# Sums of squares over the partitions on 32-column tiles and in two steps, and six token sums issued ahead of the first projection

## The chip, the cores and the metric

The kernel runs on one core of a Trainium2 chip. The metric is the device time of one execution in microseconds. In the profile PE is TensorE's matmuls, PEld its weight loads, DVE is VectorE, ACT ScalarE, POOL GpSimd and SP the engine that issues most transfers. All engines run their own queue in order and wait for each other through semaphores.

## The reference, cut to what matters

Two blocks work on 512 tokens of width 1024. The first ends in a mixture of experts whose result is added to the residual h, and then in a norm over each token; the second begins with another norm, scaled and shifted by a vector that depends on a conditioning input, and a projection. At the seam:

```python
    h = h + hier_moe(n2, ...)              # last expert unit adds its part to h
    x = rms_norm(h, final_gain)            # first block's result
    # second block, layer 0
    h2 = rms_norm_2(x, norm_g, 1e-6) * (1.0 + scale) + shift
    b_gate, c_gate, xin, z = split(h2 @ conv_w_in, 4)
```

Both norms need, for every token, a sum of squares over the 1024 features. The kernel forms the second block's input by features (features on the partitions, tokens along the free axis), so that sum runs over the 128 partitions and over eight tiles (k = 0 to 7) of 128 features each.

## The kernel before, in words

The experts are worked off in 14 units. `unit(p)` gathers tokens, runs gate, up and down matmuls, and leaves a result `O` as a high and a low part (`OT[p]`). `spread(p, t, a)` brings it back to tokens: two matmuls of 512 columns into a PSUM bank for token tile t (of 4) and half a (of 2) of the width. `add_o(a)(t, ps)`, line 692, adds that bank to `h` on DVE. For most units `combine` does all eight.

The last unit is treated otherwise. `entering`, called as its tail, does not wait for `h`: for each k a bank `HB[k]` holds the turned `h` (`so_far`, line 1276) and gets the unit's part by two more matmuls. ACT squares it with a gain into `WQ` (wq, line 1300), DVE scales it into `HS` (hs, line 1301). Behind every fourth k `first_high` has ACT cast the next projection's weights to their high part (hi, line 1321). HS and WQ are two tiles of four k each.

Then, in the body, the sum of squares over partitions: for each k and each token tile one matmul with a 128 x 128 block of WQ as the weights and a single column of ones moving, 32 in all, into four columns of one bank `pc`. DVE adds a small constant (ss, line 1429), POOL raises to the power -0.5 (line 1430), PE turns the result across the partitions (line 1433). `first_low` has DVE make the low part of the first weights (lo, line 1325).

The loop over k then multiplies hs by that factor (hs, line 1438), has ACT shift it and round it to a high part (ah, line 1439), has DVE make the low part (al, line 1440), and issues twelve matmuls: two weight tiles g, two halves m, and for each the three products high x high, high x low, low x high. In the trace they read ah,hi then al,hi then ah,lo. The four banks `ps01` collect over all k. At k = 4 and k = 6 `emit_split(2)` casts the weights of the next two jobs in two pieces each (hi on ACT line 127, lo on DVE line 128).

The order of the work is the order of the code: every engine's queue is filled as the lines are reached. `residual` is a task of small steps that `drive` runs between later matmuls; before the change it issues all eight `spread` and `add_o` of the last unit, squares h for the first block's norm and scales it. The POOL queue also issues the loads of w_mod (wm, line 367).

Of the kernel before, what the change touches and what calls it, by code (L numbers as in the profile page):

```python
# [11 lines left out]
F32 = mybir.dt.float32  # L12
# [3 lines left out]
AF = mybir.ActivationFunctionType  # L16
OP = mybir.AluOpType
# [4 lines left out]
KT = D // 128  # L22
NT = S // 128
# [7 lines left out]
NU = len(SIZES)  # L31
# [21 lines left out]
def kernel(  # L53
# [9 lines left out]
    V, A, P, T = nc.vector, nc.scalar, nc.gpsimd, nc.tensor  # L63
# [48 lines left out]
    def emit_split(cuts=1):  # L112

        j = at["split"]
        while at["load"] <= j:
            emit_load()
        _, shape, cut = specs[j]
        at["split"] = j + 1
        if cut:
            raw = loaded.pop(j)  # L120
            hi = W(shape, F32R, name="hi")
            lo = W(shape, F32R, name="lo")
            parts[j] = (hi, lo)
            n = shape[1] // cuts
            for a in range(cuts):
                r = slice(a * n, (a + 1) * n)
                A.activation(hi[:, r], raw[:, r], AF.Copy)  # L127
                V.tensor_tensor(lo[:, r], raw[:, r], hi[:, r].bitcast(F32), op=OP.subtract)  # L128
                if a == cuts - 1:
                    free(raw)  # L130
                yield
# [43 lines left out]
    h = cp.tile([128, NT, D], F32, name="h")  # L175
# [20 lines left out]
    ones = cp.tile([128, NE], F32, name="ones")  # L196
# [212 lines left out]
    def load_row(src):  # L409
        t = W([128, 2, D], name="row")  # L410
        nc.scalar.dma_start(t[:, 0, :], src.to_broadcast([128, D]))
        return t
# [277 lines left out]
    def add_o(c):  # L690
        def add(t, ps):
            V.tensor_tensor(h[:, t, c * 512:(c + 1) * 512], h[:, t, c * 512:(c + 1) * 512], ps, op=OP.add)  # L692
        return add
# [423 lines left out]
    def spread(p, t, a):  # L1117
        pb = bank()
        for n in range(2):
            mm(pb, OHT[p][:, t * 128:(t + 1) * 128], OT[p][n][:, a * 512:(a + 1) * 512], n == 0, n == 1)  # L1120
        return pb
# [157 lines left out]
    def entry_gains():  # L1279

        g = cols[:, FG:FG + 8]
        V.tensor_tensor(ent[:, 0, :], g, mods[0][1], op=OP.mult)
        V.tensor_tensor(ent[:, 1, :], g, g, op=OP.mult)
        V.tensor_scalar(ent[:, 1, :], ent[:, 1, :], EPS, 1.0 / D, op0=OP.add, op1=OP.mult)
        V.memset(ent[:, 2, :], 0.5)
        P.tensor_tensor(ent[:, 1, :], ent[:, 1, :], ent[:, 2, :], op=OP.pow)  # L1286

    def entering(p, half):

        if half == 0:  # L1290
            HS.extend(W([128, 4, 512], name="hs") for _ in range(2))
            WQ.extend(W([128, 4, 512], name="wq") for _ in range(2))
            return
        O = OT[p][2]
        for k in range(KT):
            if k not in HB:
                so_far((k,))
            for n in range(2):
                mm(HB[k], O[:, n, k * 128:(k + 1) * 128], OHT[p], False, n == 1)
            A.activation(WQ[k // 4][:, k % 4, :], HB[k], AF.Square, scale=ent[:, 1, k:k + 1])  # L1300
            V.tensor_scalar(HS[k // 4][:, k % 4, :], HB.pop(k), ent[:, 0, k:k + 1], None, op0=OP.mult)
            if k % 4 == 3:
                first_high(k // 4)

    def turned(t, x_t, r, shift, order=False):

# [7 lines left out]
    def first_high(n):  # L1314

        j = j_c[0][n]
        while at["load"] <= j:
            emit_load()
        raw, hi, lo = loaded.pop(j), W(specs[j][1], F32R, name="hi"), W(specs[j][1], F32R, name="lo")
        firsts.append((hi, lo, raw))  # L1320
        A.activation(hi, raw, AF.Copy)

    def first_low(n, r):
        hi, lo, raw = firsts[n]
        V.tensor_tensor(lo[:, r], raw[:, r], hi[:, r].bitcast(F32), op=OP.subtract)  # L1325
        if r.stop == KT:
            free(raw)
# [94 lines left out]
            free(hi, lo)  # L1422


    pc = bank()
    for k in range(KT):
        for t in range(NT):
            mm(pc[:, t:t + 1], WQ[k // 4][:, k % 4, t * 128:(t + 1) * 128], ones[:, 0:1], k + t == 0, k + t == KT + NT - 2)
    V.tensor_scalar(ss0[:, 0, 0:NT], pc[:, 0:NT], EPS * EPS, None, op0=OP.add)
    P.tensor_tensor(ss0[:, 0, 0:NT], ss0[:, 0, 0:NT], mhalf[:, :NT], op=OP.pow)  # L1430
    pr = bank()
    for t in range(NT):
        T.transpose(pr[:, t * 128:(t + 1) * 128], bc(ss0[:, 0, t:t + 1], [128, 128]), ident)
    first_low(0, slice(0, 4))
    for k in range(KT):
        x_, sh = HS[k // 4][:, k % 4, :], mods[0][0][:, k:k + 1]
        hi, lo = hT[k]
        V.tensor_tensor(x_, x_, pr, op=OP.mult)  # L1438
        A.activation(hi, x_, AF.Identity, bias=sh)  # L1439
        V.scalar_tensor_tensor(lo, x_, sh, hi.bitcast(F32), op0=OP.add, op1=OP.subtract)  # L1440
        if k in (0, 2, 4):
            first_low(*((1, slice(0, 4)), (0, slice(4, 8)), (1, slice(4, 8)))[k // 2])
        for g in range(2):
            for m in range(2):
                if k == 0:
                    ps01[g, m] = bank()
                c = slice(m * 128, (m + 1) * 128)
                w = firsts[g]
                for n, (l, r) in enumerate(passes([(w[0][:, k, c], w[1][:, k, c], hi, lo)])):
                    mm(ps01[g, m], l, r, k + n == 0, k == KT - 1 and n == 2)  # L1450
        if k in (4, 6):
            for _ in emit_split(2):
                pass
    for g in range(2):
        for m in range(2):
            ev01[g](m, ps01[g, m])
        free(*firsts[g][:2])
    free(*HS, *WQ)

    def residual():  # L1460

        p = NU - 1
        fg = load_row(final_gain[None, :])
        for t in range(NT):
            for a in range(2):
                add_o(a)(t, spread(p, t, a))
            square(h[:, t, :], ss0[:, 1, t:t + 1], D ** -0.5)
            yield
        free(OT.pop(p)[2])
        s, r = ss0[:, 1, 0:NT], ss0[:, 2, 0:NT]  # L1470
        P.tensor_scalar(s, s, EPS, None, op0=OP.add)
        P.tensor_tensor(r, s, mhalf[:, :NT], op=OP.pow)
        for t in range(NT):
            for a in range(2):
                yield
                c = slice(a * 512, (a + 1) * 512)
                V.scalar_tensor_tensor(h[:, t, c], h[:, t, c], r[:, t:t + 1], fg[:, 0, c], op0=OP.mult, op1=OP.mult)
        free(fg)
# [377 lines left out]
```

## Time and profile before

| what | value |
|---|---|
| median of 3 runs | 1481.9 us (1480.66 to 1482.22) |
| profiled execution, its own time | 1482.14 us |
| its span, first to last instruction | 1480.5 us |
| mean granted clock of TensorE | 0.978 |
| PE, PEld busy | 95%, 68% of the span |
| DVE, ACT, POOL busy | 51%, 31%, 11% |

The time is 1.64 us longer than the span; an edit inside leaves that part alone. A share is a mean over stages with different limits, so the table says only that PE is hardly ever without work. What a change is worth at one place is read from the rows of that place: what starts when, and what released it. The clock is given as a share of 2.4 GHz and has two levels, 1.00 and 0.50.

### The profile page before, as it was taken

The numbers are of one execution on the slowest core, as the hardware profiler recorded it, in microseconds if no ns is written. First come the engines' busy times: TensorE is split into PE (matmuls) and PEld (weight loads), VectorE is DVE, ScalarE is ACT, GpSimd is POOL, SyncE is SP. The second block draws the span as 40 slices with busy tenths as digits, with TensorE's granted clock in tenths as the row PEclk, the third lists the DMA queues.
The fourth block names the chain that finished last, engine by engine and source line by source line (L and its number), as shares of the span: only waits on it lengthen the run. The fifth ranks groups of instructions, "written<-read, shape, count | busy, mean of one in ns | idle before, by whom it ended". The sixth has DMA issues, their size and how long they took to land.

```text
span 1480.5 us, 19691 instructions
## 1 busy us (share of the span) xinstructions
PE 1408.9 (95%) x7919; PEld 1012.6 (68%) x7919; DVE 758.9 (51%) x1276; ACT 463.5 (31%) x656; POOL 160.5 (11%) x179
## 2 busy tenths in 40 slices
PE   6997999898999889998989999999999999999998
PEld 5876788452544234452568888888888888888876
DVE  5787746743352323242358666664444444444535
ACT  4434314220111011110233212324453453453442
POOL 1035303100000000000010000013102102112101
PEclk9999999999999899999979999999999999999999
DMA  8532563799999999999935653143123122113011
GB/s 300 192 142 87 175 256 131 318 360 420 419 420 419 419 416 420 408 418 419 359 113 175 204 170 128 57 143 105 39 61 110 54 85 90 58 58 114 30 43 58
DMA packets 102567, 310.66 MB, mean 210 GB/s; under 512 B 5128, under 2 KB 59044, under 8 KB 77892
## 3 DMA queue, kind: packets, MB, share of 16 engines
q1 hardware_dynamic: 94612, 281.36, 49.9%
q0 software_dynamic: 6704, 25.34, 4.8%
q10 hardware_dynamic: 1152, 2.62, 0.5%
q8 instruction: 64, 1.05, 0.3%
q14 instruction: 35, 0.29, 0.1%
HBM read 307.20 MB, written 2.10 MB: 209 GB/s over the span
## 4 chain that ended last, share of the span: by engine, by line
PE 54%; issue 3%; DMA 2%; DVE 2%; ACT 1%; POOL 0%; POOLq 0%; SPq 0%; DVEq 0%
PE ps L90 53%; DMA ld<-in_w_down_dram 1%; DMA ld<-in_w_up_dram 1%; PE ps L1685 1%; DVE lo L128 1%; ACT ah L1439 0%; DVE hs L1438 0%; ACT hi L127 0%; DVE lo L1325 0%; PE ps L247 0%; DVE al L1440 0%; PE ps L406 0%; PE ps L1088 0%; POOL ss L1430 0%; POOL ent L1286 0%
## 5 line engine op out<-in xcount | busy, mean ns | idle before, releaser
L90 PE MATMUL ps<-ah,hi 128*128 128x512 f32 (+1 forms) x800 | 311.7, 390 | 2.1 <-ACT ah L1439 2.1
L90 PE MATMUL ps<-al,hi 128*128 128x512 f32 (+1 forms) x800 | 306.4, 383 | 0.3 <-DVE al L1440 0.3
L90 PE MATMUL ps<-ah,lo 128*128 128x512 f32 (+1 forms) x800 | 306.2, 383 | 0.0
L90 PE MATMUL ps<-ld,XT 128*64 128x512 f32 (+1 forms) x1088 | 210.3, 614 | 14.9 <-DMA ld<-in_w_up_dram 7.8
L128 DVE TENSOR_TENSOR lo<-ld,hi 128x2048 fp32r<-128x2048 f32 (+1 forms) x73 | 161.0, 2214 | 47.7 <-ACT hi L127 47.7
L90 PEld LDWEIGHTS ps<-ah,hi 128*128 128x128 f32 x800 | 151.2, 189 | 33.5 <-issue 3.2
L90 PEld LDWEIGHTS ps<-ah,lo 128*128 128x128 f32 x800 | 151.1, 189 | 29.5
L90 PE MATMUL ps<-hi,ah 128*128 128x512 f32 (+1 forms) x456 | 171.0, 375 | 0.0
L90 PEld LDWEIGHTS ps<-al,hi 128*128 128x128 f32 x800 | 151.3, 189 | 28.6 <-DVE al L1440 1.4
L90 PEld LDWEIGHTS ps<-ld,XT 128*64 128x64 f32 (+1 forms) x1088 | 64.7, 131 | 154.8 <-issue 133.7
L90 PE MATMUL ps<-hi,al 128*128 128x512 f32 (+1 forms) x456 | 164.4, 360 | 0.0
L90 PE MATMUL ps<-lo,ah 128*128 128x512 f32 (+1 forms) x456 | 164.2, 360 | 0.0
L127 ACT ACTIVATE hi<-ld 128x2048 fp32r<-128x2048 f32 (+1 forms) x73 | 133.4, 1844 | 8.0 <-DMA ld<-in_w_in_dram 2.5
L90 PE MATMUL ps<-ld,ms 128*64 128x512 f32 (+1 forms) x544 | 109.0, 608 | 11.6 <-DMA ld<-in_w_down_dram 9.5
L1602 POOL TENSOR_TENSOR sq<-sq,rope 128x512 f32<-128x512 f32 x48 | 65.1, 1355 | 328.4 <-ACT sq L1600 328.4
L90 PEld LDWEIGHTS ps<-hi,ah 128*128 128x128 f32 x456 | 87.4, 192 | 15.4 <-issue 4.0
L90 PEld LDWEIGHTS ps<-hi,al 128*128 128x128 f32 x456 | 87.2, 191 | 13.2
L90 PEld LDWEIGHTS ps<-lo,ah 128*128 128x128 f32 x456 | 87.6, 192 | 11.3
L1112 DVE SCALAR_TENSOR_TENSOR O<-ps,wsl,O 128x512 fp32r<-128x512 f32 x28 | 20.0, 748 | 146.5 <-ACT O L1111 146.5
L692 DVE TENSOR_TENSOR h<-h,ps 128x512 f32<-128x512 f32 x128 | 79.2, 678 | 17.3 <-PE ps L90 17.3
L90 PEld LDWEIGHTS ps<-ld,ms 128*64 128x64 f32 (+1 forms) x544 | 31.4, 129 | 80.0 <-issue 58.6
L1601 DVE TENSOR_TENSOR qk<-ps,rope 128x512 f32<-128x512 f32 x48 | 33.2, 692 | 93.0 <-ACT sq L1600 93.0
(350 smaller groups left out, 1606.6 us busy)
## 6 DMA issues: line engine op xcount, KB each, us to landing
ld<-in_w_gate_dram SPq DMA_DIRECT2D x64, 1024.0 KB, 19.8
ld<-in_w_up_dram SPq DMA_DIRECT2D x64, 1024.0 KB, 12.1
ld<-in_w_down_dram SPq DMA_DIRECT2D x64, 1024.0 KB, 19.8
ld<-in_dil_w_in_dram SPq DMA_DIRECT2D x32, 1024.0 KB, 5.8
wm<-in_w_mod_dram POOLq DMA_DIRECT2D x24, 1024.0 KB, 6.8
ld<-in_conv_w_in_dram SPq DMA_DIRECT2D x16, 1024.0 KB, 8.8
ld<-in_w_in_dram SPq DMA_DIRECT2D x12, 1024.0 KB, 5.2
ld<-in_w_out_dram SPq DMA_DIRECT2D x4, 1024.0 KB
```

The costliest lines, as they stand in the source:

```text
L90: T.matmul(o, l, r, start=start, stop=stop)
L127: A.activation(hi[:, r], raw[:, r], AF.Copy)
L128: V.tensor_tensor(lo[:, r], raw[:, r], hi[:, r].bitcast(F32), op=OP.subtract)
L692: V.tensor_tensor(h[:, t, c * 512:(c + 1) * 512], h[:, t, c * 512:(c + 1) * 512], ps, op=OP.add)
L1112: V.scalar_tensor_tensor(OT[p][1][:, c], po[half], wsl[:, 0, p:p + 1], O[:, 0, c].bitcast(F32), op0=OP.mult, op1=OP.subtract)
L1601: V.tensor_tensor(dst, order(ps), order(rope[:, 0, :]), op=OP.mult)
L1602: P.tensor_tensor(sw, sw, rope[:, 1, :], op=OP.mult)
L1685: T.transpose(pt[:, j * 128:(j + 1) * 128], at_[:, i % 4, j * 128:(j + 1) * 128], ident)
```

## The change

1. `entering` no longer casts behind every fourth k; both casts come after the eighth.
2. The 32 one-column matmuls are replaced by two steps. First eight matmuls with ones (128 x 32) as weights and a k of WQ moving, 512 columns: k modulo 4 chooses one of four groups of 32 columns of the array and so 32 rows of one bank, and k = 4 to 7 add to k = 0 to 3. DVE copies that bank into the place of WQ's first k (`part`). Then four matmuls with a 128 x 128 block of `part` as weights and one column of 1/32 moving; a new memset puts that constant into `ent`.
3. The eight token sums of the last unit are kept in a list `late`. Two are issued, with their adds on DVE, behind the first step; one more behind the second; three more are copied by ACT into WQ's second tile (`keep_late`), and `residual` has POOL add them to h. The last two stay in `residual`.
4. In the loop hs and ah of k + 1 are issued ahead of al of k, and `emit_split(2)` stands at k = 5 and behind the loop.

```diff
+        V.memset(ent[:, 2, :], 1.0 / 32)
...
-            if k % 4 == 3:
-                first_high(k // 4)
+        for n in range(2):
+            first_high(n)
...
+    ps = bank()
+    for k in range(KT):
+        c = 32 * (k % 4)
+        mm(ps[c:c + 32, :], ones, WQ[k // 4][:, k % 4, :], k < 4, k >= 4)
+    part = WQ[0][:, 0, :]
+    V.tensor_copy(part, ps)
...
+    def keep_late(n):
+
+        t, a = late.pop(0)
+        kept.append((t, a, WQ[1][:, n, :]))
+        A.activation(kept[-1][2], spread(p, t, a), AF.Copy)
+
+    for _ in range(2):
+        add_late()
     pc = bank()
-    for k in range(KT):
-        for t in range(NT):
-            mm(pc[:, t:t + 1], WQ[k // 4][:, k % 4, t * 128:(t + 1) * 128], ones[:, 0:1], k + t == 0, k + t == KT + NT - 2)
+    for t in range(NT):
+        mm(pc[:, t:t + 1], part[:, t * 128:(t + 1) * 128], ent[:, 2, 1:2], t == 0, t == NT - 1)
     V.tensor_scalar(ss0[:, 0, 0:NT], pc[:, 0:NT], EPS * EPS, None, op0=OP.add)
     P.tensor_tensor(ss0[:, 0, 0:NT], ss0[:, 0, 0:NT], mhalf[:, :NT], op=OP.pow)
+    add_late()
+    for n in range(3):
+        keep_late(n)
...
+    scaled(0)
     for k in range(KT):
-        x_, sh = HS[k // 4][:, k % 4, :], mods[0][0][:, k:k + 1]
         hi, lo = hT[k]
-        V.tensor_tensor(x_, x_, pr, op=OP.mult)
-        A.activation(hi, x_, AF.Identity, bias=sh)
-        V.scalar_tensor_tensor(lo, x_, sh, hi.bitcast(F32), op0=OP.add, op1=OP.subtract)
         if k in (0, 2, 4):
             first_low(*((1, slice(0, 4)), (0, slice(4, 8)), (1, slice(4, 8)))[k // 2])
+        if k + 1 < KT:
+            scaled(k + 1)
+        V.scalar_tensor_tensor(lo, HS[k // 4][:, k % 4, :], mods[0][0][:, k:k + 1], hi.bitcast(F32), op0=OP.add,
+                               op1=OP.subtract)
...
-        if k in (4, 6):
+        if k == 5:
             for _ in emit_split(2):
                 pass
+    for _ in emit_split(2):
+        pass
...
+        while late:
+            add_late()
+        for t, a, y in kept:
+            c = slice(a * 512, (a + 1) * 512)
+            P.tensor_tensor(h[:, t, c], h[:, t, c], y, op=OP.add)
+        yield
```

On PE, from the last block of `entering` to the first matmuls of the loop (O and oht are the unit's result and its one-hot map, ident turns a tile), the kernel before has:

```order
L90 MATMUL ps<-oht,O 128x512 x2
L90 MATMUL ps<-ones,wq 128x1 x32
L1433 MATMUL ps<-ident,ss_2005 128x128 x4
L90 MATMUL ps<-ah,hi 128x512
L90 MATMUL ps<-al,hi 128x512
```

and the changed kernel, from the same matmul on:

```order
L90 MATMUL ps<-oht,O 128x512 x2
L90 MATMUL ps<-wq,ones 32x512 x8
L90 MATMUL ps<-O,oht 128x512 x4
L90 MATMUL ps<-ent,wq 128x1 x4
L90 MATMUL ps<-O,oht 128x512 x8
L1458 MATMUL ps<-ident,ss_2005 128x128 x4
L90 MATMUL ps<-ah,hi 128x512
L90 MATMUL ps<-al,hi 128x512
```

The twelve matmuls on O,oht moved here from the job behind the loop; four of them are left there.

On DVE, from the hs of `entering` to the first al, the kernel before has:

```order
L1301 TENSOR_SCALAR hs<-ps,ent 128x512 x8
L1429 TENSOR_SCALAR ss_2005<-ps 128x4
L1325 TENSOR_TENSOR lo<-ld,hi 128x1024
L1438 TENSOR_TENSOR hs<-hs,ps 128x512
L1440 SCALAR_TENSOR_TENSOR al<-hs,mod_274,ah 128x512
```

and the changed kernel (COPY is the copy into `part`, L692 the adds to h):

```order
L1302 TENSOR_SCALAR hs<-ps,ent 128x512 x8
L1434 COPY wq<-ps 128x512
L692 TENSOR_TENSOR h<-h,ps 128x512 x2
L1451 TENSOR_SCALAR ss_2005<-ps 128x4
L692 TENSOR_TENSOR h<-h,ps 128x512
L1326 TENSOR_TENSOR lo<-ld,hi 128x1024
L1463 TENSOR_TENSOR hs<-hs,ps 128x512
L1326 TENSOR_TENSOR lo<-ld,hi 128x1024
L1463 TENSOR_TENSOR hs<-hs,ps 128x512
L1473 SCALAR_TENSOR_TENSOR al<-hs,mod_274,ah 128x512
```

Between the small operation on the sums (ss) and the first al there are now an add, a second lo and a second hs. On POOL the three adds (L1499) stand right behind the power (L1452) and ahead of three loads of w_mod; the order of SP's loads is as before.

## Rows read from the trace of the kernel before

**Rows 1.** The page, busy time of PE: us, share of span, instructions.

```profile
PE 1408.9 (95%) x7919; PEld 1012.6 (68%) x7919; DVE 758.9 (51%) x1276; ACT 463.5 (31%) x656; POOL 160.5 (11%) x179
```

**Rows 2.** Waits of PE, 733 to 776, then 776 on: total, times, longest us.

```profile
PE ps L1433 <- POOL ss L1430: 2.3, 1, 2.3
...
PE ps L1685 <- DVE at L1677: 3.4, 1, 3.4
```

**Rows 3.** Timeline at the entry: start, length, engine, line, count, [idle before].

```profile
729.37 2.42 ACT L1300 ACTIVATE wq<-ps,ent 128x512 f32<-128x512 f32 x4
...
730.09 2.72 DVE L1301 TENSOR_SCALAR hs<-ps,ent 128x512 f32<-128x512 f32 x4
...
731.66 1.93 ACT L1321 ACTIVATE hi<-ld 128x2048 fp32r<-128x2048 f32 x1
...
733.24 11.47 PE L90 MATMUL ps<-ones,wq 128*128 128x1 f32 x64
```

**Rows 4.** Timeline, the chain from the sums to the loop.

```profile
744.85 1.22 DVE L1325 TENSOR_TENSOR lo<-ld,hi 128x1024 fp32r<-128x1024 f32 x1
744.98 1.96 POOL L1430 TENSOR_TENSOR ss<-ss,mhalf 128x4 f32<-128x4 f32 x1 [43.47 <-DVE ss L1429]
...
747.00 1.11 PE L1433 MATMUL ps<-ident,ss 128*128 128x128 f32 x4 [2.29 <-POOL ss L1430]
...
748.88 0.72 ACT L1439 ACTIVATE ah<-hs,mod 128x512 fp32r<-128x512 f32 x1 [11.18 <-DVE hs L1438]
749.63 0.75 DVE L1440 SCALAR_TENSOR_TENSOR al<-hs,mod,ah 128x512 fp32r<-128x512 f32 x1 [0.79 <-ACT ah L1439]
...
750.43 0.79 PE L90 MATMUL ps<-al,hi 128*128 128x512 f32 x1
```

**Rows 5.** Timeline, k = 7 of the loop on PE.

```profile
772.86 0.50 PE L90 MATMUL ps<-ah,hi 128*128 128x512 f32 x1 [0.54 <-ACT ah L1439]
...
773.65 0.50 PE L90 MATMUL ps<-al,hi 128*128 128x512 f32 x1 [0.29 <-DVE al L1440]
...
776.07 0.39 PE L90 MATMUL ps<-ah,lo 128*128 128x512 f32 x1
```

**Rows 6.** Windows: length, busy (records) by engine, granted clock, DMA share, GB/s.

```profile
734.00:736.00 2.00, 2.00 (x18) 2.00 (x18) 1.80 (x3) 2.00 (x5) 0.00 (x0) 0.90 1.06 339
754.00:756.00 2.00, 2.00 (x6) 1.60 (x5) 1.21 (x3) 0.72 (x1) 0.00 (x0) 0.50 0.00 0
756.00:758.00 2.00, 2.00 (x10) 1.58 (x10) 1.52 (x2) 0.44 (x1) 0.00 (x0) 0.98 0.00 0
```

**Rows 7.** Timeline, down matmuls of two units, 32 and 64 columns.

```profile
523.71 7.07 PE L90 MATMUL ps<-ld,ms 128*32 128x512 f32 x64
...
721.52 7.09 PE L90 MATMUL ps<-ld,ms 128*64 128x512 f32 x32 [0.69 <-ACT ms L1089]
```

**Rows 8.** Timeline, two token sums in the job behind the loop.

```profile
779.02 1.07 PE L90 MATMUL ps<-O,oht 128*128 128x512 f32 x4
...
779.92 0.39 PE L90 MATMUL ps<-ah,hi 128*128 128x512 f32 x1
```

**Rows 9.** Timeline on POOL, and line L1676: shortest, median, longest in ns.

```profile
793.51 1.04 POOL L1472 TENSOR_TENSOR ss<-ss,mhalf 128x4 f32<-128x4 f32 x1
...
1006.35 1.30 POOL L1602 TENSOR_TENSOR sq<-sq,rope 128x512 f32<-128x512 f32 x1 [1.59 <-ACT sq L1600]
...
L1676 DVE TENSOR_TENSOR at<-at x32: 269/272/1310, 1063.4 to 1430.7; 128x128 f32<-128x128 f32 x32
```

**Rows 10.** Timeline of PE, then windows, at two other gaps.

```profile
560.12 0.66 PE L1088 MATMUL ps<-ident,ms 128*128 128x128 f32 x4 [1.18 <-DVE ms L1080]
561.46 1.09 PE L90 MATMUL ps<-ld,ms 128*64 128x512 f32 x2 [0.69 <-ACT ms L1089]
...
562.00:564.00 2.00, 2.00 (x6) 0.49 (x4) 0.00 (x0) 0.00 (x0) 0.00 (x0) 0.50 1.02 422
...
720.00:722.00 2.00, 1.14 (x7) 0.62 (x8) 0.12 (x1) 0.60 (x1) 0.00 (x0) 1.00 0.98 393
```

More of the change, by code (lines that the diff above doesn't have):

```diff
@@ L1422, in half_tokens, with add_late @@
             free(hi, lo)
+    p = NU - 1
+    late = [(t, a) for t in range(NT) for a in range(2)]
+    kept = []
+    ps = bank()
[4 more added lines that the diff above has]
+    V.tensor_copy(part, ps)
+    def add_late():
+        t, a = late.pop(0)
+        add_o(a)(t, spread(p, t, a))
+    def keep_late(n):
+        t, a = late.pop(0)
+        kept.append((t, a, WQ[1][:, n, :]))
+        A.activation(kept[-1][2], spread(p, t, a), AF.Copy)
+    for _ in range(2):
+        add_late()
     pc = bank()
-    for k in range(KT):
-        for t in range(NT):
-            mm(pc[:, t:t + 1], WQ[k // 4][:, k % 4, t * 128:(t + 1) * 128], ones[:, 0:1], k + t == 0, k + t == KT + NT - 2)
+    for t in range(NT):
+        mm(pc[:, t:t + 1], part[:, t * 128:(t + 1) * 128], ent[:, 2, 1:2], t == 0, t == NT - 1)
     V.tensor_scalar(ss0[:, 0, 0:NT], pc[:, 0:NT], EPS * EPS, None, op0=OP.add)
     P.tensor_tensor(ss0[:, 0, 0:NT], ss0[:, 0, 0:NT], mhalf[:, :NT], op=OP.pow)
+    add_late()
+    for n in range(3):
+        keep_late(n)
     pr = bank()
@@ L1434, with scaled @@
     first_low(0, slice(0, 4))
+    def scaled(k):
+        x_ = HS[k // 4][:, k % 4, :]
+        V.tensor_tensor(x_, x_, pr, op=OP.mult)
+        A.activation(hT[k][0], x_, AF.Identity, bias=mods[0][0][:, k:k + 1])
+    scaled(0)
     for k in range(KT):
-        x_, sh = HS[k // 4][:, k % 4, :], mods[0][0][:, k:k + 1]
         hi, lo = hT[k]
-        V.tensor_tensor(x_, x_, pr, op=OP.mult)
-        A.activation(hi, x_, AF.Identity, bias=sh)
-        V.scalar_tensor_tensor(lo, x_, sh, hi.bitcast(F32), op0=OP.add, op1=OP.subtract)
         if k in (0, 2, 4):
             first_low(*((1, slice(0, 4)), (0, slice(4, 8)), (1, slice(4, 8)))[k // 2])
+        if k + 1 < KT:
+            scaled(k + 1)
+        V.scalar_tensor_tensor(lo, HS[k // 4][:, k % 4, :], mods[0][0][:, k:k + 1], hi.bitcast(F32), op0=OP.add,
+                               op1=OP.subtract)
         for g in range(2):
@@ L1457 @@
         free(*firsts[g][:2])
-    free(*HS, *WQ)
     def residual():
-        p = NU - 1
         fg = load_row(final_gain[None, :])
+        while late:
[4 more added lines that the diff above has]
+        yield
+        free(*HS, *WQ)
         for t in range(NT):
-            for a in range(2):
-                add_o(a)(t, spread(p, t, a))
             square(h[:, t, :], ss0[:, 1, t:t + 1], D ** -0.5)
```

## The prediction

> **What bounds the kernel now.** I read the shares of the engines first. PE is busy for 1408.9 us of the 1480.5 us span [rows 1], so an edit is worth what it takes off PE's row. Then I read what ended PE's idle time on either side of the place that the diff touches. From 733 to 776 us its longest wait is 2.3 us for the power on POOL; after 776 us the page of waits has a single entry for PE, 3.4 us in all [rows 2]. Behind the edited place nothing but PE's own order sets the end, and what is won there should reach the end whole. The transfers have no say: POOL's and SP's loads of that stage are not waited for by PE at all.
>
> The place itself is the entry of the second block. Eight squares (wq) and eight scaled copies (hs) come from ACT and DVE, and then PE spends 11.47 us on 64 records of one column each, two for each of the 32 matmuls [rows 3]. What follows is a chain with nothing beside it on PE: power, turn, hs, ah, first matmul of k = 0, then al and the second matmul at 750.43 [rows 4]. From there PE runs one behind another until a last stall at k = 7 (0.54 and 0.29 us), and the last of 96 matmuls starts at 776.07 [rows 5]. Meanwhile the granted clock has fallen: 0.90 on the mean of 734 to 736 us, 0.50 (1.2 GHz) at 754 to 756, 0.98 in the next 2 us [rows 6]. The fall comes while PE does the one-column matmuls, and the rise some 5.4 us after the dense work began. At half the clock those 5.4 us cost 2.7.
>
> **The change part by part.** Times below are on the clock of the profiled run; up to 733 us the two programs are the same but for one small constant, which hides in the unit before.
>
> *Feeding.* ACT does the eight squares in a row and casts the first weights after. Squares pass at 2.42 / 4 = 0.605 us, casts at 1.93 [rows 3], so the last four squares no longer stand behind a cast. The last block's matmuls end where the series of ones starts, 733.24, so the last square ends about 734.3. The eight hs follow on DVE at 2.72 / 4 = 0.68: 730.09 + 5.44 = 735.53.
>
> *Sums on 32 columns.* Eight matmuls of 512 columns, two records each, take the place of the 32. The nearest row has this very form: 64 records on 32-column tiles in 7.07 us, against 32 on 64-column tiles in 7.09 [rows 7]. So 0.110 us a record, four tiles at once, and 16 records take 1.77. Starting at 733.24, with the last four waiting for their squares, they end at about 735.3, just before hs does. If they did not run side by side they would take four times as long, 7.1 us. I take 1.77.
>
> The Trainium skill ("TensorE: Matmul & The Clock Gate", Part 3, "Measured speedup vs the span model") lists a speedup of 2.38 for three column tiles, which is 79% of the ideal. By that the 16 records would take an estimated 2.2 us instead of 1.77, and the sum below would be some 0.2 us poorer, because hs hides the rest.
>
> *Copy and second step.* DVE copies the sums from PSUM behind hs; at the price of an hs, 0.68, it ends at 736.2. The second step is four matmuls of one column, eight records. The old series gives 11.47 / 64 = 0.18 a record, mostly at the low clock, and nearer to 0.11 at the high one [18 records in 2 us, rows 6]: 0.9 to 1.45 us. I take 0.9, since PE comes from dense work; it ends at 737.2. DVE has put two adds to h before the small TENSOR_SCALAR that reads the result (1.36 us at 0.68 each), so that one runs at 737.6 and not at 737.2: 0.4 us that the adds cost.
>
> *Power.* 1.96 us in this place [rows 4], beside a DVE lo that started 0.13 us earlier; 1.04 us for the same form alone [rows 9]. In the new order lo comes after the power, so I take 1.04: 737.8 to 738.85.
>
> *Token sums in the waits.* Six of the eight are now issued here, two before the second step and four after it. Four such matmuls hold PE for 0.90 us, 779.02 to 779.92 [rows 8], 0.225 each. The first two sums fill the wait for the copy. The other four (1.8 us) last until 739.0, 0.1 us longer than the power: they cost that 0.1 and nothing more. Later PE is rid of twelve matmuls, 12 x 0.225 = **2.7 us**, in a stage where it never waits. ACT's three copies fit behind the casts (0.6 each, done before 740.2). POOL's three adds stand ahead of the w_mod loads in its queue; those wait for slots that DVE and PE give back only in the loop behind, so they lose nothing.
>
> *From the turn to the second matmul.* Turn 739.0 to 739.6 (1.11 us at half the clock [rows 4], so 0.6). DVE must finish lo first: it starts at 738.5 and meets the power, then hs at 740.1 and ah behind it, and the first matmul of k = 0 at 741.5. The second matmul needs al of k = 0, and the new order puts lo (1.22) and hs of k = 1 (0.68) ahead of it: 740.75 + 1.22 + 0.68 + 0.75 = 743.4. In this stretch POOL's three adds run, at 1.30 us each [rows 9]. The rows show that they matter: L1676, a DVE operation with both inputs in SBUF, takes 0.27 us as a rule and 1.31 once [rows 9], when POOL was at work. lo and al are of that kind. Each would wait some 0.6 us for the add then running: 744.6. Bounds: 743.4 with no meeting, 746.0 with two whole adds in the way. I take **744.6**, which is **5.8 us** earlier than 750.43.
>
> *The loop.* 95 matmuls at 0.225 are 21.4 us. DVE's work for eight k is about as much: eight times 0.68 + 0.75, four lo at 1.22 and two splits of two such pieces, 21.2 us. But hs is now made one k ahead, and the second split comes behind the loop. From al of k = 0 to al of k = 7 DVE has six hs, seven al, two lo and one split in its queue, 14.2 us, so the last al is there at 759, or 760 with another wait for POOL; PE wants it after 85 matmuls, at 763.7. So the stall of rows 5 goes: 0.54 ahead of k = 7, and 3.21 - 11 x 0.225 = 0.73 within it, **1.3 us**.
>
> *The clock.* From 739.6 to 744.6 PE does one matmul. Two places show what such a gap does. With a turn between gaps of 1.18 and 0.69 us the clock was at 0.50 from 562 on, though dense work had begun at 561.46; at 720 to 722, with a similar turn and a wait of the same 0.69 us, it stayed at 1.00 [rows 7, 10]. The new gap is longer than either, so I let it fall, and lose between 0 and 2.7 us (that of before), at 2.2, against 2.7 now: **0.5 us** gained.
>
> The Trainium skill ("TensorE: Matmul & The Clock Gate", Part 4) says that a transpose does not count as work for the clock as other matmuls do. By that the turn would be no help in the gap, and a clock that stays up would be less likely still; the row at 720 shows a turn without a fall.
>
> **Sum.** 5.8 + 1.3 + 0.5 + 2.7 = 10.3 us less than the profiled 1482.14, or 1471.84; the median of the runs is 0.24 lower than that run, so **1471.6**.
>
> **The rivals.**
> (a) *The clock stays up and POOL is not in the way.* For it: the row at 720. Against it: the longer gap. It gains 2.2 + 1.2 more: 1468.2. Half of it (one of the two) lies in between.
> (b) *The tiles do not run side by side*, so the change does not do what it says. 7.1 us in place of 1.77, of which 0.2 is hidden by hs: 5.1 us lost, 1476.7. Against it: rows 7.
> (c) *DVE becomes the bound at the head of the loop.* lo and al each wait for a whole add of POOL, the power takes 1.96, and the one-column step 1.45. That is 1.4 + 0.9 + 0.5 = 2.8 us: 1474.4. For it: L1676; against it: adds and lo are out of step.
> (d) *Slower: the low clock lasts.* If DVE feeds the loop in such a rhythm that PE keeps pausing, the clock stays at 1.2 GHz, and each matmul costs 0.225 more. I count 2.2 / 0.225, some 10 of them, already. It takes 10.3 / 0.225 = 46 more, half of the loop, to eat the gain; if all 96 run so, the other 86 add 19.4 us: 1491.0. Against it: in the trace of before the clock rose in this loop though it began with a stall.
>
> **How the numbers follow.** Forecast 0.55, (a) 0.18, (c) 0.14, (b) 0.08, (d) 0.05. The range reaches to (a) and over (c) to near (b): 1467.8 to 1475.8. The measurement can tell about 0.2%, 3 us, from no change. Only (d) falls outside faster: of it I give 0.02 to the same and 0.03 to slower. Faster 0.95.
>
> **What would show it.** In the new profile: 16 records on 32-column tiles within 2.2 us; one copy, then the one-column step of some 0.9 us; the second matmul of k = 0 near 744.6; no PE wait at k = 7; twelve fewer matmuls on O between 776 and 792; lo or al stretched beside POOL's adds. The forecast is wrong if the sums take 7 us, if al of k = 0 comes after 747, if the clock stays at 0.50 beyond 752, or if PE shows a wait after 776 that is not there now.

## The result and the profile after

The changed kernel takes 1472.2 us (median of 4 runs, 1470.4 to 1474.2) against 1482.1 for the kernel before beside it (1480.7 to 1482.4): a ratio of 0.9936, with a 95% interval of 0.9919 to 0.9953. A second comparison on another chip gave 1473.1 against 1482.2, ratio 0.9940 (0.9928 to 0.9952). The forecast was 1471.6, with a range of 1467.8 to 1475.8.

The profiled run took 1474.2 us, its span 1472.5. First the page (busy us, share, instructions), to be read against [rows 1]: PE has lost 8.5 us and 40 instructions.

```profile
PE 1400.4 (95%) x7879; PEld 1002.2 (68%) x7879; DVE 758.7 (52%) x1275; ACT 465.2 (32%) x659; POOL 166.3 (11%) x182
```

The waits of PE from 733 to 776 us, and then from 776 us on (total, times, longest), stand against the two lines of [rows 2]. The wait for POOL's power is gone. What is left ahead of the loop are the first ah and the first al. The one late wait is as it was.

```profile
PE ps L90 <- DVE al L1473: 1.9, 1, 1.9
PE ps L90 <- ACT ah L1464: 1.5, 1, 1.5
...
PE ps L1721 <- DVE at L1713: 3.4, 1, 3.4
```

The timeline of the entry (start, length, engine, line, operation, count, [idle before]) answers [rows 3 and 4]:

```profile
736.52 1.92 PE L90 MATMUL ps<-wq,ones 128*32 128x512 f32 x16
...
738.59 0.69 DVE L1434 COPY wq<-ps 128x512 f32<-128x512 f32 x1
739.20 1.27 DVE L692 TENSOR_TENSOR h<-h,ps 128x512 f32<-128x512 f32 x2
739.41 0.98 PE L90 MATMUL ps<-ent,wq 128*128 128x1 f32 x8
740.25 2.09 PE L90 MATMUL ps<-O,oht 128*128 128x512 f32 x8
740.42 0.16 DVE L1451 TENSOR_SCALAR ss<-ps 128x4 f32<-128x4 f32 x1
740.66 1.01 POOL L1452 TENSOR_TENSOR ss<-ss,mhalf 128x4 f32<-128x4 f32 x1 [36.13 <-DVE ss L1451]
...
741.59 1.22 DVE L1326 TENSOR_TENSOR lo<-ld,hi 128x1024 fp32r<-128x1024 f32 x1
...
742.18 0.60 PE L1458 MATMUL ps<-ident,ss 128*128 128x128 f32 x4
742.19 5.64 POOL L1499 TENSOR_TENSOR h<-h,wq 128x512 f32<-128x512 f32 x3 [0.52 <-ACT wq L1444]
742.82 0.69 DVE L1463 TENSOR_TENSOR hs<-hs,ps 128x512 f32<-128x512 f32 x1
743.42 1.60 DVE L1326 TENSOR_TENSOR lo<-ld,hi 128x1024 fp32r<-128x1024 f32 x1
...
744.31 0.49 PE L90 MATMUL ps<-ah,hi 128*128 128x512 f32 x1 [1.53 <-ACT ah L1464]
744.94 0.67 DVE L1463 TENSOR_TENSOR hs<-hs,ps 128x512 f32<-128x512 f32 x1
745.54 1.15 DVE L1473 SCALAR_TENSOR_TENSOR al<-hs,mod,ah 128x512 fp32r<-128x512 f32 x1
...
746.75 0.80 PE L90 MATMUL ps<-al,hi 128*128 128x512 f32 x1 [1.94 <-DVE al L1473]
```

The chain has kept its members and lost its length. Beside the three POOL adds (5.64 us where three alone are 3 x 1.30, [rows 9]) the lo has 1.60 us and the al 1.15, where [rows 4] have 1.22 and 0.75. The lo of 741.59 is the first one; it starts as the power ends and keeps its 1.22.

The windows (length, busy by engine, granted clock in the third column from the end) show the clock fall once here, at about 745.6 us, and rise at about 752.4. In the kernel before it was down through the one-column matmuls as well, until 756 [rows 6].

```profile
744.00:746.00 2.00, 0.49 (x1) 0.19 (x1) 2.00 (x3) 0.61 (x2) 2.00 (x1) 0.90 0.52 177
746.00:748.00 2.00, 1.25 (x3) 1.06 (x4) 2.00 (x3) 1.05 (x2) 1.83 (x2) 0.50 0.00 0
...
752.00:754.00 2.00, 2.00 (x9) 1.61 (x8) 2.00 (x4) 0.33 (x2) 0.00 (x0) 0.89 0.35 74
754.00:756.00 2.00, 2.00 (x11) 1.64 (x10) 1.69 (x3) 1.47 (x3) 0.00 (x0) 1.00 1.03 339
```

**One clock for all runs.** The first sum starts at 733.24 us in the profile of before, at 736.52 in this one, and at 733.17 in a second profile of the same changed kernel, though the code ahead of it is the same but for a memset and the place of ACT's casts. In the two profiles of the changed kernel the lag goes with the clock, far ahead of this place. Two windows of the first profile, then of the second:

```profile
150.00:154.00 4.00, 4.00 (x15) 2.63 (x16) 0.69 (x1) 0.60 (x1) 1.20 (x2) 0.50 0.00 0
292.00:296.00 4.00, 4.00 (x14) 1.18 (x12) 1.76 (x14) 0.43 (x3) 0.00 (x0) 0.62 1.02 416
```

```profile
150.00:154.00 4.00, 4.00 (x23) 2.60 (x19) 0.69 (x1) 0.60 (x1) 1.20 (x2) 0.78 0.00 0
292.00:296.00 4.00, 4.00 (x22) 1.19 (x18) 0.51 (x4) 0.00 (x0) 0.00 (x0) 1.00 1.00 412
```

ACT's row at line 611 starts 1.6 us later in the first (157.2 against 155.6), its row at line 976 3.3 us later (300.7 against 297.4), and the first sum 3.3 us later too. So all that follows is counted from the first sum. *m2* is the second matmul of k = 0, *loop* the matmul behind the last of the 96, *rest* the run's own time less the start of the first sum. *Low* is how long the clock stood at 0.50 in the stretch from the sums to the loop, worked out from windows of 2 us. Two profiles of the changed kernel agree to 0.01 us in the first three columns, and all four programs that were profiled twice do so at m2. Behind m2 the clock can part two profiles of one program: e_both by 0.95 at the loop's end, u_loop by 1.17 in the rest. That is still sharper than medians, whose runs mostly lie 3 to 4 us apart. The medians come from several chips; the kernel before, run beside each set, had 1482.1 to 1482.3.

| kernel | m2 | loop | rest | low | median, us |
|---|---|---|---|---|---|
| before | 17.19 | 43.06 | 748.90 | 20.5 | 1482.1 |
| changed | 10.23 | 34.56 | 737.68 | 6.8 | 1472.2 |
| a_again (changed, second) | 10.24 | 34.56 | 737.68 | 6.8 | 1473.1 |
| x1_sums | 10.84 | 36.71 | 743.61 | 6.8 | 1478.1 |
| u_late | 10.52 | 34.17 | 740.00 | 10.2 | 1475.9 |
| u_loop | 9.25 | 36.21 | 740.27 | none | 1476.8 |
| loop_again (second profile) | 9.26 | 36.20 | 739.10 | 3.4 | 1472.6, one run |
| s_serial | 15.62 | 40.12 | 743.19 | 6.8 | 1479.4 |
| e_dve | 9.43 | 32.49 | 735.55 | 3.4 | 1469.9 |
| e_al | 9.26 | 32.58 | 736.80 | none | 1473.8 |
| al_again (second profile) | 9.25 | 32.57 | 736.66 | none | 1472.9, one run |
| e_both | 8.58 | 31.77 | 734.84 | 3.4 | 1469.9 |
| both_again | 8.58 | 30.82 | 733.94 | none | 1470.8 |
| e_fill | 8.57 | 30.81 | 732.92 | none | 1466.8 |

By this clock the change gains 748.90 - 737.68 = 11.2 us: 7.0 up to m2, 1.5 from there to the end of the loop (25.87 against 24.33), and 2.7 behind it.

### The profile page after: what moved, and what is told of

Its sections match the earlier page's. It is cut to its first block, busy times and chain, and to the rows that moved or that the text cites. A ratio compares the mean times of both kernels' runs of the same rounds, so it can differ in the third digit from the quotient of the medians.

```text
span 1472.5 us, 19622 instructions
## 1 busy us (share of the span) xinstructions
PE 1400.4 (95%) x7879; PEld 1002.2 (68%) x7879; DVE 758.7 (52%) x1275; ACT 465.2 (32%) x659; POOL 166.3 (11%) x182
## 4 chain that ended last, share of the span: by engine, by line
PE 58%; DMA 3%; DVE 1%; issue 1%; ACT 1%; POOLq 0%; POOL 0%; DVEq 0%; SPq 0%
PE ps L90 56%; DMA ld<-in_w_down_dram 1%; DMA ld<-in_w_up_dram 1%; PE ps L1721 1%; DVE lo L128 0%; ACT hi L127 0%; PE ps L247 0%; DVE lo L1326 0%; PE ps L1088 0%; PE ps L406 0%; DVE ms L1080 0%; ACT L1656 0%; ACT ms L1089 0%; DVE al L1473 0%; DVE sq L1745 0%
## 5 line engine op out<-in xcount | busy, mean ns | idle before, releaser
L90 PEld LDWEIGHTS ps<-lo,ah 128*128 128x128 f32 x456 | 87.3, 191 | 11.2
L692 DVE TENSOR_TENSOR h<-h,ps 128x512 f32<-128x512 f32 x125 | 77.5, 677 | 14.9 <-PE ps L90 14.9
```

## Experiments

Theory: the gain is the shorter chain to the second matmul (sums, copy, second step), the sums by token that found a place in PE's waits, and the loop that no longer stalls. What stands in the way of more is POOL's three adds beside lo and al, the order that puts a lo and an hs ahead of the first al, and the clock. No run moves ACT's casts alone. Rivals: that the parts are worth something only together, that hs hides the sums whatever their length, and that the clock does it all.

**One part alone: the two-step sums (x1_sums).** The kernel before with the new sums and nothing else:

```diff
+        V.memset(ent[:, 2, :], 1.0 / 32)
...
-        for t in range(NT):
-            mm(pc[:, t:t + 1], WQ[k // 4][:, k % 4, t * 128:(t + 1) * 128], ones[:, 0:1], ...)
+        c = 32 * (k % 4)
+        mm(ps[c:c + 32, :], ones, WQ[k // 4][:, k % 4, :], k < 4, k >= 4)
+    V.tensor_copy(part, ps)
+    for t in range(NT):
+        mm(pc[:, t:t + 1], part[:, t * 128:(t + 1) * 128], ent[:, 2, 1:2], t == 0, t == NT - 1)
```

> The kernel before with the two-step sums alone: token sums, casts and loop stay as they were. My theory: the chain gets shorter by what the 11.47 us of one-column matmuls lose, so the second matmul of k = 0 comes 10.0 to 11.0 us after the first of the sums instead of 17.2, the stall of 0.8 us at k = 7 stays, and the time is 6 to 7 us below before (1475 to 1476). Rival (the sums were hidden behind the rest of the chain, and the moved token sums and the new loop order bring most of the gain): 0 to 3 us below before.

Measured: 1478.1 us, ratio 0.9969 (0.9957 to 0.9982); second matmul at 10.84, between the 10 and 11 expected. The loop ends 6.35 earlier, but only 5.3 are left on the rest, and the median gains 4.2 where 6 to 7 were expected; the rival, at most 3, fails too. The 1.06 between loop and rest is lost near the end, where the clock stood low for 6.8 us in this profile and for 3.4 in that of before (more on this at e_al). The timeline:

```profile
737.28 3.66 PE L90 MATMUL ps<-wq,ones 128*32 128x512 f32 x16
...
742.93 1.23 DVE L1326 TENSOR_TENSOR lo<-ld,hi 128x1024 fp32r<-128x1024 f32 x1
743.06 1.96 POOL L1436 TENSOR_TENSOR ss<-ss,mhalf 128x4 f32<-128x4 f32 x1 [36.82 <-DVE ss L1435]
745.08 0.72 PE L1439 MATMUL ps<-ident,ss 128*128 128x128 f32 x4 [2.30 <-POOL ss L1436]
```

Two things that the full change repairs are still there. The sums last 3.66 us, since the last four squares stand behind a cast, and the power takes 1.96 beside a lo that started 0.13 us before it. The loop from m2 on is as long as before (25.87), but not by the same parts. A k of twelve matmuls takes 2.72 us when nothing holds it up. Before, k = 5, 6 and 7 took 1.55 more than that together; here k = 4 to 7 took 2.23 more, and the head of the loop, where the clock was low for less of the time, took 0.69 less. What the faster head won, the loop lost again in waiting for DVE and ACT.

**One part undone: the token sums (u_late).** The changed kernel with all eight sums left in the job behind the loop:

```diff
-    for _ in range(2):
-        add_late()
...
-    add_late()
-    for n in range(3):
-        keep_late(n)
...
+            for a in range(2):
+                add_late()
```

> The changed kernel with all eight token sums left behind the loop. My theory: PE gets the twelve matmuls back (2.7 us); on the other side the power starts some 0.4 us earlier, and lo and al of k = 0 no longer meet POOL's adds (0.8 us), so the time is 1 to 2 us above the changed kernel and 8 to 9 us below before (1473 to 1474). Rival (the sums in the waits are wholly free): 2.7 us above the changed kernel, with the second matmul of k = 0 where the changed kernel has it, 10.2 us after the first of the sums.

Measured: 1475.9 us, above the 1473 to 1474 of the theory, and 2.3 us more on the rest (740.00 against 737.68), between theory (1 to 2) and rival (2.7). The power did not start 0.4 earlier (4.15 after the first sum, against 4.14), so the adds to h had cost it nothing. The second matmul came 0.3 later, not the same, but the parts are larger and nearly cancel:

```profile
739.49 1.23 DVE L1326 TENSOR_TENSOR lo<-ld,hi 128x1024 fp32r<-128x1024 f32 x1
739.56 2.03 POOL L1450 TENSOR_TENSOR ss<-ss,mhalf 128x4 f32<-128x4 f32 x1 [35.21 <-DVE ss L1449]
741.64 1.11 PE L1453 MATMUL ps<-ident,ss 128*128 128x128 f32 x4 [2.37 <-POOL ss L1450]
...
744.29 0.79 PE L90 MATMUL ps<-ah,hi 128*128 128x512 f32 x1 [1.53 <-ACT ah L1459]
745.13 0.75 DVE L1468 SCALAR_TENSOR_TENSOR al<-hs,mod,ah 128x512 fp32r<-128x512 f32 x1
```

Without the add to h between them, lo starts just ahead of the power, which takes 2.03 instead of 1.01; without the sums PE is idle, and in this profile the turn ran at half the clock, 1.11 instead of 0.60. So the first matmul comes 1.1 us later. Against that al is 0.75 us long, since no adds run on POOL, and most is given back. The 2.3 is 0.3 at m2, less 0.7 in the loop, where the clock rose earlier (some 4.3 us behind m2, against 5.7), and 2.7 for twelve matmuls that stand behind it again.

**One part undone: the loop's order (u_loop, loop_again).** The changed kernel with hs, ah and al of each k at the head of that k, and the splits at k = 4 and 6, as before:

```diff
-        if k + 1 < KT:
-            scaled(k + 1)
...
+        V.tensor_tensor(x_, x_, pr, op=OP.mult)
+        A.activation(hi, x_, AF.Identity, bias=sh)
+        V.scalar_tensor_tensor(lo, x_, sh, hi.bitcast(F32), op0=OP.add, op1=OP.subtract)
...
-        if k == 5:
+        if k in (4, 6):
```

> The changed kernel with the loop's order of before (hs and ah of k behind al of k - 1, splits at k = 4 and 6). My theory: al of k = 0 has no lo and no hs of k = 1 ahead of it, so the second matmul comes 1.9 to 2.3 us earlier than in the changed kernel, but the stalls on ah and al at k = 6 and 7 come back (1.3 us, or more since PE starts the loop with less lead): within 1 us of the changed kernel. Rival (the new loop order is what the gain is made of): 2 us or more above the changed kernel.

> A second profile of the changed kernel with the loop order of before, whose first showed no fall of the clock with the second matmul at 9.25 us. If what PE does decides alone: none again, loop end at 36.2 us. Otherwise a fall, with the same rows around it and a later loop end.

Measured: 1476.8 us, then 1472.6 in the single run. The second matmul came a whole microsecond *earlier* than in the changed kernel (9.25), because al now stands right behind ah, though not the 1.9 to 2.3 expected: al met POOL's adds and took 1.42; yet the loop ended 1.65 later in both profiles. The waits of PE there in u_loop (changed kernel: one 1.5 and one 1.9):

```profile
PE ps L90 <- ACT ah L1470: 3.5, 4, 1.5
PE ps L90 <- DVE al L1471: 1.8, 4, 1.0
PE ps L90 <- DVE lo L1326: 0.4, 1, 0.4
```

So the new order is worth 1.65 us at the loop's end, against the theory; the first median, 3.8 or more above the changed kernel, is the rival's, and the second is a single run. Up to the loop's end the two profiles differ in one thing: in the first the clock never fell here, in the second it stood at 0.50 for 3.4 us, and the loop ended at 36.21 and 36.20. In this loop, in which PE waits for DVE and ACT, the slow clock cost nothing.

**One cost taken away: the adds on POOL (e_dve).**

```diff
-            P.tensor_tensor(h[:, t, c], h[:, t, c], y, op=OP.add)
+            V.tensor_tensor(h[:, t, c], h[:, t, c], y, op=OP.add)
```

> The changed kernel with the three kept parts added to h by DVE, at the same place in the program (a task step behind the loop), instead of by POOL. My theory: lo of k = 0's second weights and al of k = 0 take 1.22 and 0.75 us again instead of 1.60 and 1.15, and the second matmul of k = 0 comes 0.8 us earlier; DVE's three adds of 0.7 us lie in a stage where PE does not wait for it: 0.5 to 0.8 us below the changed kernel. Rival (POOL's adds do not matter to DVE, the long lo and al have another cause): lo and al stay long, and the time is that of the changed kernel.

Measured: 1469.9 us, ratio 0.9914 (0.9900 to 0.9927), 2.3 to 3.2 below the two medians of the changed kernel, where 0.5 to 0.8 was expected. The second matmul came 0.80 us earlier, as expected. lo and al have their own lengths again:

```profile
743.49 1.22 DVE L1326 TENSOR_TENSOR lo<-ld,hi 128x1024 fp32r<-128x1024 f32 x1
...
745.22 0.75 DVE L1473 SCALAR_TENSOR_TENSOR al<-hs,mod,ah 128x512 fp32r<-128x512 f32 x1
...
746.02 0.80 PE L90 MATMUL ps<-al,hi 128*128 128x512 f32 x1 [1.14 <-DVE al L1473]
```

The meeting itself costs 0.38 + 0.40 = 0.78 us. The loop ended 2.07 earlier, and the other 1.3 is the clock, which stood low for 3.4 us instead of 6.8. That the move of the adds brought this 1.3 too is not shown: e_both, below, fell once and not once with the same program. DVE had room for the three adds behind the loop: from the loop's end on the run takes 703.06 us, and the changed kernel 703.12.

**The order ahead of the first al (e_al, e_both), and the changed kernel beside them (a_again).** At k = 0 alone, al is issued ahead of the lo and of the hs of k = 1; e_both has the adds on DVE too.

```diff
+        if k == 0:
+            low()
         if k in (0, 2, 4):
             first_low(...)
         if k + 1 < KT:
             scaled(k + 1)
+        if k:
+            low()
```

> The changed kernel itself once more, on the same chip as the three that follow, so that differences of 1 to 2 us can be read. Expected 1470.4 to 1474.2 us, as in the first comparison; second matmul of k = 0 some 10.2 us after the first sum, granted clock 0.50 from about 1 us before it to 5.5 us after it.

> The changed kernel with al of k = 0 issued ahead of the lo and the hs of k = 1; the three kept adds stay on POOL. Theory: al meets POOL's first add and takes 1.1 to 1.4 us, as it did in the run with the loop of before; second matmul at 9.0 to 9.3 us after the first sum, clock up; lo is stretched to 1.6 to 2.3 and holds up al of k = 1 by about 1 us, so the loop ends at 32 to 32.5, and the time is 2 us below the changed kernel. Rival (order is worth nothing so long as POOL's adds run, since DVE has the same work to do before k = 1 in either order): second matmul earlier, but loop end at 34 to 34.6 and the time within 0.7 us of the changed kernel.

> A second profile of the kernel with al of k = 0 first and the kept adds on POOL, whose first showed no fall of the clock with the second matmul 9.26 us after the first sum. If what PE does decides alone: none again, loop end at 32.6 us. If when the stretch comes has a part: a fall of some 3 to 7 us with the same rows around it, and a loop end 1.7 to 3 us later.

> The changed kernel with the three kept adds on DVE instead of POOL, and with al of k = 0 issued ahead of the lo and the hs of k = 1. Theory (what is left of the wait for al is half POOL, half order, and the clock falls only because of its length): al stands 0.75 us long right behind ah, so the second matmul of k = 0 comes 8.6 us after the first sum, against 9.43 with the adds alone moved and 10.23 in the changed kernel. The clock stays at 1.00 through the loop, as it did in the run with the loop of before, where that matmul came at 9.25. The loop then ends about 31 us after the first sum, against 32.5 and 34.6: 1.5 us below the run with the adds alone moved, 1468.4 us. Rival (the clock falls whatever the gap, because PE does next to nothing between the turn and that matmul): the second matmul at 8.6 too, but the clock at 0.50 for some 3 to 5 us behind, loop end at 32 to 33, and 1469.5 to 1470.5 us. Second rival: al of k = 1 is now late, since lo and hs stand between the two, and PE waits 1 us or more for it: then the clock is up and a wait for al of k = 1 is in the rows.

> The kernel with al of k = 0 first and the kept adds on DVE once more, to stand beside the filled one on the same chip: 1468 to 1471 us; second matmul 8.58 us after the first sum. If the fall of the clock in this place hangs on what PE does there and on nothing else, it is there again, 3.4 us long. If it hangs on when the stretch comes, this run may show none or a longer one, with the same rows of PE around it.

Measured: a_again 1473.1, e_al 1473.8, e_both 1469.9 us; on another chip both_again 1470.8 and al_again 1472.9 (single). The second matmul stands where the theory put it, 9.26 with the adds on POOL and 8.58 without.

In e_al the adds were met all the same (timeline):

```profile
744.67 1.43 DVE L1472 SCALAR_TENSOR_TENSOR al<-hs,mod,ah 128x512 fp32r<-128x512 f32 x1 [0.79 <-ACT ah L1464]
...
746.02 2.30 DVE L1326 TENSOR_TENSOR lo<-ld,hi 128x1024 fp32r<-128x1024 f32 x1
```

That is 0.68 and 1.08 us on the two, more than in the changed kernel. The loop ended 2.0 us earlier in both profiles (32.58 and 32.57), near the 32 to 32.5 expected, and still the time is not 2 us lower: the medians are 0.8 apart the other way, less than the spread of the runs. In the profiles 1.1 of the 2.0 is lost again 650 us later, behind PE's last wait, where the clock falls once more. The windows from 1418 to 1430 us, of the changed kernel and then of e_al:

```profile
1418.00:1430.00 12.00, 8.62 (x41) 6.94 (x40) 3.68 (x6) 3.30 (x4) 0.00 (x0) 0.86 0.00 0
```

```profile
1418.00:1430.00 12.00, 8.62 (x38) 7.04 (x38) 2.97 (x4) 1.73 (x3) 0.00 (x0) 0.72 0.00 0
```

12 x 0.14 x 2 = 3.4 us at half the clock against 12 x 0.28 x 2 = 6.7. al_again has 0.72 there as well. The wait is the same 3.4 us in all three; only the moment at which it comes has moved. That the edit brings this about is not shown, for one program has both: u_loop, then loop_again, from 1420 to 1432.

```profile
1420.00:1432.00 12.00, 8.62 (x33) 6.88 (x32) 3.67 (x5) 3.04 (x4) 0.00 (x0) 0.72 0.00 0
```

```profile
1420.00:1432.00 12.00, 9.70 (x50) 8.47 (x51) 3.76 (x6) 1.12 (x2) 0.00 (x0) 0.86 0.00 0
```

This explains why the two have the same loop end and rests 1.17 apart. In the table, rest less loop is about 703 us where the twelve matmuls were moved (702.1 in e_fill, with four more) and 705.8 where they were not. It is about 1 us more in exactly the four profiles whose stretch here is 6.8: x1_sums 706.90, u_loop 704.06, e_al 704.22, al_again 704.09.

With e_both the rival came near in the first profile (the clock fell for 3.4 us, loop end 31.77 where it said 32 to 33), and the theory in the second (clock up, 30.82), though neither median came down to the theory's 1468.4. Windows of e_both, then of both_again, around the second matmul (at 742.65 and 745.58):

```profile
742.00:744.00 2.00, 1.71 (x4) 1.22 (x5) 2.00 (x3) 0.00 (x0) 0.00 (x0) 0.63 0.30 100
744.00:746.00 2.00, 2.00 (x6) 1.54 (x6) 1.81 (x4) 1.34 (x2) 0.00 (x0) 0.52 0.00 0
746.00:748.00 2.00, 2.00 (x11) 1.62 (x10) 2.00 (x3) 0.36 (x1) 0.00 (x0) 1.00 0.00 0
```

```profile
744.00:746.00 2.00, 0.92 (x3) 0.56 (x4) 1.22 (x2) 0.72 (x1) 0.00 (x0) 1.00 0.78 271
746.00:748.00 2.00, 2.00 (x11) 1.61 (x9) 1.86 (x3) 0.70 (x2) 0.00 (x0) 1.00 0.00 0
```

The program is the same, and so are the rows of PE up to m2. Once the clock fell for 3.4 us and once it did not. The loop gained only 0.95 of a possible 1.7 from the fast clock, because k = 1 then took 3.29 us and not 2.73: its al was late, and DVE became the limit for a moment.

**The tiles side by side (s_serial).** All eight sums on one tile of 32 columns:

```diff
-        c = 32 * (k % 4)
-        mm(ps[c:c + 32, :], ones, WQ[k // 4][:, k % 4, :], k < 4, k >= 4)
+        mm(ps[0:32, :], ones, WQ[k // 4][:, k % 4, :], k == 0, k == KT - 1)
```

> The changed kernel with all eight matmuls of the sums on one tile of 32 columns (rows 0 to 31 of the result) instead of four tiles in turn; copy and one-column step on those 32 rows. Theory (the four tiles run side by side, which is why 16 records take 1.92 us): they take 16 x 0.44 = 7.1 us here, one after another, and the power, the turn and the loop come 5 us later: 5 us above the changed kernel, about 1477. Rival (a 32-column matmul is short whatever tile it is on, or hs hides it): 2 to 3.5 us for the sums and 0 to 1.5 us above the changed kernel.

Measured: 1479.4 us, ratio to before 0.9978 (0.9969 to 0.9987).

```profile
736.09 7.05 PE L90 MATMUL ps<-wq,ones 128*32 128x512 f32 x16
```

7.05 us where four tiles take 1.92, so the theory holds to 0.05. The copy starts 5.0 us later (7.09 after the first sum against 2.07): the 5.13 of the sums less the little that hs hides. The two token sums ahead of the second step no longer fit into the wait for the copy and hold that step up by another 0.2. The second matmul came 5.4 us later (15.62 against 10.24) and the rest is 5.5 longer.

**The gap filled (e_fill).** e_both with the last two token sums behind the turn, their copies behind the first ah:

```diff
     first_low(0, slice(0, 4))
+    last = [late.pop(0) for _ in range(2)]
+    last = [(t, a, spread(p, t, a)) for t, a in last]
...
     scaled(0)
+    for (t, a, s), y in zip(last, (WQ[1][:, 3, :], WQ[0][:, 1, :])):
+        A.activation(y, s, AF.Copy)
+        kept.append((t, a, y))
```

> The kernel with al of k = 0 first and the kept adds on DVE, and the last two token sums (four matmuls, 0.9 us) issued on PE right behind the turn, their copies on ACT behind the first ah, their adds kept with the others. Theory (the granted clock falls there because PE has next to nothing between the turn and the second matmul): PE's idle time ahead of the first matmul shrinks from 1.53 to 0.6 us, the clock stays at 1.00 in the loop, which ends 1.7 us earlier (30.1 us after the first sum instead of 31.8), and the job behind the loop has four matmuls fewer, 0.9 us: 2.6 us below the kernel without the fill, 1467.3 us. Rival (the length of this gap does not decide: in two runs with a second matmul as late as 9.25 the clock stayed up, and in one at 8.58 it fell): the clock falls all the same, only the 0.9 us are won, 1469.0 us.

Measured: 1466.8 us (1466.5 to 1467.8), ratio 0.9897 (0.9882 to 0.9912), the fastest of all. The four matmuls lie in the wait for ah, which shrinks from 1.53 to 0.60:

```profile
739.38 0.60 PE L1458 MATMUL ps<-ident,ss 128*128 128x128 f32 x4
739.73 1.17 PE L90 MATMUL ps<-O,oht 128*128 128x512 f32 x4
...
741.51 0.49 PE L90 MATMUL ps<-ah,hi 128*128 128x512 f32 x1 [0.60 <-ACT ah L1466]
```

The clock stayed at 1.00, but it did so in both_again without the fill, so this run does not show that the fill holds it up, and its time near the theory's 1467.3 is no proof of the theory. Against both_again the loop ends at the same time (30.81 and 30.82, not the 30.1 expected, since al of k = 1 is late here too) and the rest is 1.0 us shorter, nearly all of it the 0.9 of four matmuls. The medians are 3.9 apart. In the profiles the rest of the gap lies ahead of the first sum (733.72 against 737.00), in code that is the same in both. There the clock stood low for 44.4 us in both_again and for 30.7 in e_fill, summed from windows of 2 us. None of e_fill's four runs was above 1467.8; why its clock fell less is open.

## Why the prediction was right, point by point

- **Sums**: forecast 1.77 us, measured 1.92, and end before hs does (2.12 us after the first sum; forecast 2.29). Right; s_serial shows what the tiles side by side are worth.
- **Copy and second step**: 0.69 and 0.98, for 0.68 and 0.9. The 0.4 us put down for the two adds to h did not come: the small ss behind them starts 0.03 us after the second step ends (739.41 + 0.98), so the power started at 4.14 instead of 4.56. u_late, without these adds, has 4.15.
- **Power**: 1.01, as forecast (1.04). x1_sums and u_late, where lo starts ahead of it, have 1.96 and 2.03. That its place behind an add to h decides this is shown by u_late.
- **Token sums in the waits**: the four behind the second step held the turn up by some 0.4 us instead of 0.1 (power ends at 741.67, the sums at about 742.1), and their twelve matmuls are gone later, 12 x 0.227 = 2.7. Right, with 0.3 to the bad. In u_late, without them, the turn ran at the low clock; that they keep it up rests on this one profile.
- **First matmul**: 7.79, forecast 8.26. The turn starts only 0.1 earlier than forecast (5.66 against 5.76), since the token sums took back what the adds had not cost. The other 0.4 is the first lo: the forecast let it meet the power and hold up hs by 0.5 us, and it starts as the power ends and is done with the turn, so that hs starts at once.
- **Second matmul**: 10.23, forecast 11.36 (744.6 on the clock of before; 743.5 if the 3.28 us by which this profile's first sum is later are taken off). The gain of the chain is 17.19 - 10.23 = 7.0, not 5.8. POOL's adds were in the way as the step said, but for 0.78 us and not 1.2 (e_dve). 0.47 came from the first matmul, 0.42 from this, and the rest from DVE, whose operations start 0.08 us before the row ahead of them ends (hs 742.82 + 0.69, lo at 743.42).
- **The stall at k = 7**: gone, as forecast: the waits of PE show none. It was 1.55 us and not 1.3. Rows 5 show k = 7 alone; counted over whole k, the kernel before lost 0.13 at k = 5, 0.70 at k = 6 and 0.72 at k = 7.
- **The clock**: it fell, as forecast; the dense work then ran at 1.2 GHz from 746.75 to about 752.4, which is some 5.7 x 0.5 = 2.8 us and not 2.2. Before, it was the same: by [rows 6] the clock rose at about 756.1, 5.65 us behind the second matmul at 750.43, where the prediction counted 5.4, so 2.8 and not 2.7. That is no gain at all, where 0.5 had been put down. This is a term that was mis-sized.
- **The sum**: 7.0 + 1.5 + 2.7 = 11.2 against the forecast 10.3, and the medians show 9.8 and, in the second comparison, 9.1. The chain was set 1.1 too low and the loop with its clock 0.3 too high (stall 0.25 too low, clock 0.5 too high). In the profiled run 3.28 of the 11.2 are lost ahead of the first sum, whose start differs by some 4 us between profiles of programs that are the same up to there; what part of this is in the medians no profile can say. So that the time was hit to 0.6 us is partly luck: the sum itself was 0.9 us short.
- **The rivals**: none came. Of (a) neither half: the clock fell, and POOL was in the way. both_again, in whose profile neither holds, has 3.7 us less on the rest than the changed kernel, near the 3.4 of (a), though al also stands further forward there. (b) is what s_serial shows, 5.4 us for 5.1 worked out. (c) had its mechanism, lo and al stretched, but for less than even the forecast had, and not the long power. (d) was nowhere: the clock rose within 6 us of the dense work. None of the signs of a wrong forecast came either: counted on the clock of before, al of k = 0 starts at 742.3 and the clock is up from about 749.2.
- **A reading**: the prediction says that L1676 took 1.31 us once. It did so twice, at 1211.44 and 1320.09, each time beside POOL's L1602, so the case for the meeting was somewhat better than it was put.

The Trainium skill's rule ("SBUF — State Buffer", section "Who interferes with whom") says that a DVE operation with two inputs in SBUF contends with a GpSimd operation that reads SBUF, that the contention is an exclusive lock, and that the order of issue decides which of the two is blocked. The trace agrees in both directions: the power, 0.13 us behind a lo of 1.23, took 1.96 instead of 1.01, and lo beside the adds took up to 2.30 instead of 1.22. That lo, in e_al, starts at 746.02, while POOL's third add runs until 747.24, and it ends 1.08 us behind that add.

By the Trainium skill's 2.38 for three column tiles ("TensorE: Matmul & The Clock Gate", Part 3, "Measured speedup vs the span model") the prediction had also set an estimated 2.2 us for the sums. The runs show 7.05 us on one tile and 1.92 on four, 3.7 times, so the row was the better guide.

## What to carry to other kernels

Small sums over partitions that stand on the path belong in a few wide matmuls on 32-column tiles, with a tiny second step, and not in many one-column matmuls. When a chain is shortened, look at what runs on POOL beside DVE's operations with two SBUF inputs, in both directions: moving three adds to DVE, though DVE was on the path and POOL had time, took 0.8 us off the wait for the first al. And compare parts from an anchor inside the trace, with the clock beside them: every program that was profiled twice had its second matmul at the same place to 0.01 us, while the medians of two comparisons lay 0.8 apart. A term behind a clock that may fall needs a range and not a number.

## What the runs showed of the hardware

- With the same program and the same rows of PE ahead of it, the granted clock fell in one profile and not in the other, in e_both (low for 3.4 us, then not) and in u_loop (not, then for 3.4 us). The length of PE's gap does not settle it: it stayed at 1.00 with the second matmul at 9.26 and fell with it at 8.58. What decides stays open.
- A low stretch costs half its length where PE is the limit (2.8 us of 5.7 in the changed kernel) and cost nothing where PE waits for DVE and ACT (u_loop: loop ends of 36.20 and 36.21 with and without).
- Behind one and the same wait of 3.4 us near the end the clock stood low for 3.4 us in ten profiles and for 6.8 in four, and one program has both (u_loop 6.8, loop_again 3.4). In e_al a gain of 2.0 us in the loop so came out as 0.9.
- The start of the first sum differs by some 4 us between profiles, and in the changed kernel's pair the lag goes with where the clock stood low before it (0.50 against 0.78 from 150 to 154 us, 0.62 against 1.00 from 292 to 296).
